# The weights of q and of the output projection: split into high and low halves beside the Fourier transform instead of ahead of it, through DRAM

## Chip, core and metric

One NeuronCore of a Trainium2 chip runs the whole kernel. The metric is the time of one execution on the device, in microseconds (us); lower is better. Engines are named as in the profile: PE is TensorE, DVE is VectorE, ACT is ScalarE, POOL is GpSimd, SP is the engine whose queue issues nearly all DMAs. Every engine works through its own instruction list strictly in order, so an instruction that waits holds up all that stand behind it on the same engine.

## What is computed

One layer of a hybrid block over 2048 latent tokens of width 1024 (a Fourier branch and a retention branch beside each other). Cut to what matters:

```python
h = modulate(rms_norm(x, g_pre), shift, scale)            # shift, scale, gate from silu(c) @ w_ada
f_in, f_gate, q, k, v, r_gate = split(h @ w_in)           # six projections of 512 columns each
q, k = axial_rotary(q) * QK_SCALE, axial_rotary(k)
ret = bidirectional_retention(q, k, v, decay, fwd_state, bwd_state)     # chunks of 128 tokens
mixed = real(fft2(f_in per group of 128 channels)); yf = (mixed @ w_fourier) * silu(f_gate)
yr = group_norm(ret) * gn_gain * silu(r_gate)
out = x + gate * rms_norm(concat(yf, yr) @ w_out, g_post)
```

## The kernel before

The latent tokens are 16 chunks of 128 (c = 0 to 15), two to a tile (t = 0 to 7). Products need more precision than one pass of PE gives, so every operand x is split into hi (x rounded, a copy on ACT) and lo (x - hi, a subtraction on DVE, some on POOL), and a product is three matmuls: hi\*hi, hi\*lo, lo\*hi (`proj_kt`, lines 180 to 182). Splitting a weight costs a load, an ACT copy and a subtraction; a split weight is twice as large as the raw one.

The program runs in stages:

- **Tiles 1 to 7** (about 75 to 320 us): k, v and, for tiles 1 to 3, r_gate of each chunk; k^T, v and the running state go to DRAM (`d_st`). The order within this stage is a scheduler's. Work that is not urgent is put between the chunks by hand: `gate_acc` (the sum over c for the output gate, GG), `decay_tables`, the splits of the Fourier weights (`jobs`: B11, B21, T1, T2, then T3, B22, T4), and `w_ahead`: twelve pieces of the weights of q and of the output projection (`wq`, `wo0`, `wo1`) are loaded, split and stored split in DRAM (`d_w`), two pieces after each of the chunks 2 to 7. So they are done with tile 3.
- **`f_tile` 0 to 7** (320 to 495 us): f_in and f_gate by a Strassen-like scheme of seven products for each pair of chunks. PE's order is written by hand. `h_raw` loads a pair's rows, `h_comb` adds and splits them. In `f_tile(4)` `gate_fin` finishes GG with two matmuls.
- **The transform** (495 to 580 us): order written by hand on all engines. Four classes k of four groups g: `T` (`cls_T`, 12 matmuls into pT) and `Y` (`cls_y`, 6 matmuls, then the gating on POOL). ACT makes Th and DVE makes Tl of each T, which Y reads. Between them PE is filled with `fill`: quarters (6 matmuls) of the r_gate projection of the chunks 15 down to 8, which `rg_rest` generates; their operands (`rgh`) come from DRAM into the four buffers of pool `w4`, so a chunk's load waits until an earlier chunk is done. `pull` issues steps of the next class's operands (`ops_pair`, `ops_even`).
- **q and retention** (from 576 us): q of tile 7 and 6 (`q_steps`), retention of chunk 15, 14, ..., then in `chunk_step` one chunk after the other with the output projection two chunks behind (`out_steps`: o[0], o[1] with `wo0`; o[2], o[3] with `wo1`). `load_sd` fetches k^T, v and states of a chunk, `spill` writes the gated Fourier rows of a group to DRAM. `w_get` loads the split `wq` (before tile 7's q) and `wo0`, `wo1` (between the steps).

Tiles share pools: `units` (20 buffers of 8 KB a partition), `w4` (4 of 4 KB), `w2` (16 of 2 KB, taken by `wk`). A new tile waits until all readers of its buffer's last owner are done, and on SP such a wait holds every DMA behind it.

Of the kernel before, what the change touches and what calls it, by code (L numbers as in the profile page):

```python
# [15 lines left out]
P = 128  # L16
# [15 lines left out]
def hymba_kernel(ctx: ExitStack, tc: tile.TileContext, a: dict, out: bass.AP):  # L32
# [805 lines left out]

    d_w = {n: drm.tile([4, P, 2, 2, 512], F32, name=f"d_{n}") for n in ("wq", "wo0", "wo1")}
    gains = [None] * 4 + [gn_col[:, i:i + 1] for i in range(4)]  # L840

    def w_ahead(n, u):
        src, col = {"wq": (a["w_in"], 1024), "wo0": (a["w_out"], 0), "wo1": (a["w_out"], 512)}[n]
        raw = w4.tile([P, 2, 512], F32, tag="w4", name="wa")
        nc.sync.dma_start(out=raw, in_=src[u * 256:(u + 1) * 256, col:col + 512]
                          .rearrange("(k p) n -> p k n", p=P))
        d = unit([P, 2, 2, 512], F32R, "wahl")
        if n == "wq" or u < 2:
            hl_split(d, raw)
        else:  # L850
            for j in range(2):
                w_split([d], j, raw[:, j, :], gains[2 * u + j])
        nc.sync.dma_start(out=d_w[n][u], in_=d.bitcast(F32))

    def w_get(n, wu, us=range(4)):
        for u in us:
            nc.sync.dma_start(out=wu[u].bitcast(F32), in_=d_w[n][u])

    ahead = [(n, u) for n in ("wq", "wo0", "wo1") for u in range(4)]

    jobs = {(4, 1): [lambda: b_plain("B11", 0, 0)], (5, 1): [lambda: b_plain("B21", 1, 0)],
            (6, 0): [b_T1], (6, 1): [b_T2]}

    for t in range(1, NT - 1):
        hi, lo = hls.pop(t)
        for b in range(2):
# [19 lines left out]
            for n, u in ahead[:2]:  # L886
                w_ahead(n, u)
            ahead = ahead[2:]
# [7 lines left out]
    toks = [slice(b * P, (b + 1) * P) for b in range(2)]  # L896
    b_T3()
# [8 lines left out]
    h_comb(0)  # L906
# [60 lines left out]
    def f_tile(t):  # L967
# [35 lines left out]
        if t == 4:  # L1003
            gate_fin()
# [405 lines left out]
    def rg_load(c):  # L1410
        rgh[c] = [w4.tile([P, KT, P], F32R, tag="w4", name="rgh") for _ in range(2)]
# [36 lines left out]
    with tc.manual_schedule(engines={ENG.PE, ENG.DVE, ENG.Activation, ENG.Pool, ENG.SP}):  # L1448
# [5 lines left out]
        fg_sum(NT - 1, 0, Z, last["u2"])  # L1454
        bg.append(gen1(ops_pair(2)))
        pull(9)
        for g in range(4):
            sg.append(unit([P, SEQ], F32, f"sg{g}"))
            for c in FB[NT - 1]:
                s_ = slice((c - 7) * P, c * P)  # L1460
                nc.sync.dma_start(out=sg[g][:, s_], in_=d_sg[g][:, s_])
        fill(4)
        fg_T(NT - 1, 1)
        fg_T(NT - 1, 0)
        fill(2)
# [3 lines left out]
        bg.append(gen1(ops_pair(1)))  # L1469
# [20 lines left out]
        pull(9)  # L1490
        load_h(7, 0)
        load_h(7, 1)
        load_tab(3)
        load_sd(N1)
        dec.append(wk([P, NH, P], "DT"))
        dec.append(unit([P, 2, NH, P], F32, "dec"))
        nc.sync.dma_start(out=dec[0], in_=d_dec[:, 0])
        nc.sync.dma_start(out=dec[1], in_=d_dec[:, 1:3])
        load_h(6, 0)
        load_h(6, 1)  # L1500
        for g in range(4):
            pend.append((2, g, T(2, g)))
            Y(*pend.pop(0))
            pull(1)
            if g == 0:
                bg.append(gen1(ops_even()))
        for f in q_steps(7):
            if pend:
                Y(*pend.pop(0))
            f()  # L1510
            pull(1)
        pull(9)
# [3 lines left out]
        split_h(6, 1)
        load_sd(N1 - 1)
        wo_u = [w_units(f"wo{j}") for j in range(2)]
        q2 = q_steps(6)
# [200 lines left out]
```

## Time and profile before

| | us |
|---|---|
| median of three runs | 938.44 (937.55 to 939.31) |
| the profiled execution, its own time | 939.14 |
| its span, first to last instruction | 937.3 |
| PE busy | 888.9 (95%) |
| VectorE, ScalarE, GpSimd busy | 583.6, 353.8, 280.4 |

The span and the instruction times are those of one execution under the profiler; its own time is 1.84 us more than its span. PE is busy for 95% of it, so what can be won without changing the arithmetic is PE's idle time and the time in which PE was granted the lower clock.

### The profile page before, as it was taken

The page shows a single profiled execution, that of the slowest core. Times are in us where ns is not written, and L with a number is a line of the kernel's source. Part 1 is how long each engine was busy: PE and PEld are TensorE (multiplying, and loading weights), DVE is VectorE, ACT ScalarE, POOL GpSimd, SP SyncE. Part 2 cuts the span into 40 slices and gives each one's busy share as a digit, 9 for nine tenths or more (in the row PEclk, how much of TensorE's full clock was granted, in tenths as well). Part 3 has the DMA queues.
Part 4 walks back from the last instruction along what each step waited for, and adds up shares of the span by engine and source line. Part 5 has one row for each costly group of instructions (what it writes and reads, how often), then busy time and mean ns, then how long its engine had stood idle before and what let it go on. Part 6 is the DMA issues. An engine that isn't in the chain of part 4 may idle for free.

```text
span 937.3 us, 13777 instructions
## 1 busy us (share of the span) xinstructions
PE 888.9 (95%) x4996; PEld 760.0 (81%) x4996; DVE 583.6 (62%) x1126; ACT 353.8 (38%) x691; POOL 280.4 (30%) x333
## 2 busy tenths in 40 slices
PE   7899999999998799999998899987999999999997
PEld 6678888888787678887886789976898989989885
DVE  3555675585799795476527254773666867677552
ACT  3444754344644553333323233221234233433331
POOL 2106321321456310000001147442343424334342
PEclk8899999999999999999999899999999999999999
DMA  8938987999999732234269589599445464243412
GB/s 303 389 121 328 337 314 299 389 381 391 357 377 371 224 113 68 79 85 118 79 229 355 153 268 413 195 359 381 155 146 180 162 188 170 91 147 113 168 58 90
DMA packets 109939, 214.25 MB, mean 229 GB/s; under 512 B 7728, under 2 KB 58160, under 8 KB 99248
## 3 DMA queue, kind: packets, MB, share of 16 engines
q1 hardware_dynamic: 108000, 207.08, 62.2%
q0 software_dynamic: 576, 4.19, 1.2%
q10 hardware_dynamic: 1296, 2.10, 0.6%
q8 instruction: 39, 0.64, 0.3%
q14 instruction: 28, 0.23, 0.1%
HBM read 141.78 MB, written 71.57 MB: 228 GB/s over the span
## 4 chain that ended last, share of the span: by engine, by line
PE 54%; DMA 7%; DVE 3%; POOL 2%; issue 2%; ACT 0%; SPq 0%; DVEq 0%; POOLq 0%; ACTq 0%
PE pX L926 8%; PE pout L180 6%; PE pout L182 6%; PE pout L181 6%; PE pZ L926 4%; PE pq L1203 3%; PE pq L1204 3%; PE pq L1205 3%; DMA wo<-d_wo 3%; PE pY L926 2%; DMA sd<-d_st 2%; PE psc L1245 2%; PE pr L182 2%; DMA rgh<-d_hl 1%; PE pr L180 1%
## 5 line engine op out<-in xcount | busy, mean ns | idle before, releaser
L180 PE MATMUL pout<-wo,y 128*128 128x512 f32 x256 | 103.0, 402 | 5.7 <-DMA wo<-d_wo 5.7
L182 PE MATMUL pout<-wo,y 128*128 128x512 f32 x256 | 100.4, 392 | 0.0
L181 PE MATMUL pout<-wo,y 128*128 128x512 f32 x256 | 100.2, 391 | 0.0
L1203 PE MATMUL pq<-hq,wq 128*128 128x256 f32 x256 | 74.2, 290 | 0.4 <-DMA hq<-d_hl 0.4
L1204 PE MATMUL pq<-hq,wq 128*128 128x256 f32 x256 | 73.3, 286 | 0.0
L1205 PE MATMUL pq<-hq,wq 128*128 128x256 f32 x256 | 73.2, 286 | 0.0
L926 PE MATMUL pX<-T,S 128*128 128x512 f32 x276 | 67.4, 393 | 1.5 <-DVE fg L58 1.5
L242 POOL TENSOR_TENSOR vd<-v,dk 128x256 f32<-128x256 f32 x64 | 54.0, 872 | 42.6 <-ACT v L634 21.8
L180 PEld LDWEIGHTS pout<-wo,y 128*128 128x128 f32 x256 | 48.3, 189 | 16.8 <-DMA wo<-d_wo 7.8
L206 POOL TENSOR_TENSOR ka<-ka,kb 128x512 f32<-128x512 f32 x16 | 31.4, 1966 | 102.0 <-DVE kb L58 87.5
L926 PEld LDWEIGHTS pX<-T,S 128*128 128x128 f32 x276 | 51.1, 188 | 12.3 <-DVE fg L58 1.9
L182 PEld LDWEIGHTS pout<-wo,y 128*128 128x128 f32 x256 | 48.3, 189 | 10.6
L1335 ACT ACTIVATE t<-pout 128x512 f32<-128x512 f32 x32 | 19.1, 597 | 98.6 <-PE pout L182 71.7
L181 PEld LDWEIGHTS pout<-wo,y 128*128 128x128 f32 x256 | 48.5, 189 | 9.0
L1203 PEld LDWEIGHTS pq<-hq,wq 128*128 128x128 f32 x256 | 50.0, 195 | 0.8 <-issue 0.6
L1204 PEld LDWEIGHTS pq<-hq,wq 128*128 128x128 f32 x256 | 50.0, 195 | 0.2
L1205 PEld LDWEIGHTS pq<-hq,wq 128*128 128x128 f32 x256 | 49.9, 195 | 0.0
L1363 POOL TENSOR_TENSOR xo<-xo,t 128x512 f32<-128x512 f32 x30 | 43.2, 1455 | 21.5 <-DMA xo<-in_x 10.2
L1038 POOL DMA_DIRECT2D tab<-in_tabs x4 | 2.6, 643 | 151.5 <-PE pX L926 151.5
L180 PE MATMUL pv<-wv,hhix 128*128 128x512 f32 x112 | 44.8, 400 | 0.0
L180 PE MATMUL pk<-wk,hhix 128*128 128x512 f32 x112 | 44.1, 393 | 0.0
L182 PE MATMUL pk<-wk,hlox 128*128 128x512 f32 x112 | 43.6, 391 | 0.2 <-DVE hlox L55 0.2
(316 smaller groups left out, 2432.0 us busy)
## 6 DMA issues: line engine op xcount, KB each, us to landing
sd<-d_st SPq DMA_DIRECT2D x16, 1024.0 KB, 6.3
braw<-in_w_in SPq DMA_DIRECT2D x18, 512.0 KB, 8.4
ada<-in_ada_ss SPq DMA_DIRECT2D x8, 1024.0 KB, 12.9
d_wo<-wahl SPq DMA_DIRECT2D x8, 1024.0 KB, 10.3
hr<-d_h SPq DMA_DIRECT2D x32, 256.0 KB, 4.4
rgh<-d_hl SPq DMA_DIRECT2D x16, 512.0 KB, 8.2
wo<-d_wo SPq DMA_DIRECT2D x8, 1024.0 KB, 10.2
out<-xo SPq DMA_DIRECT2D x32, 256.0 KB, 2.1
```

Source lines behind the costliest of these rows:

```text
L180: mm(o, hi[:, kt, tok], whi, start=first, stop=False)
L181: mm(o, hi[:, kt, tok], wlo, start=False, stop=False)
L182: mm(o, lo[:, kt, tok], whi, start=False, stop=last)
L206: nc.gpsimd.tensor_tensor(out=ra, in0=ra, in1=rb.rearrange("p h a f -> p h (a f)"), op=ALU.add)
L242: nc.gpsimd.tensor_tensor(out=t[:, :, i, :], in0=v[:, hs, :], in1=d[:, hs].unsqueeze(2).to_broadcast([P, 2, P]), op=ALU.mult)
L926: mm(o, A[:, x, kt, :], w, start=(first and kt + i == 0), stop=(kt + i == 5), skip_group_check=not first)
L1203: mm(o, whi, h[:, 0, kt % 4], start=(kt == 0), stop=False)
L1204: mm(o, wlo, h[:, 0, kt % 4], start=False, stop=False)
L1205: mm(o, whi, h[:, 1, kt % 4], start=False, stop=(kt == KT - 1))
L1245: mm(psc[:, h * P:(h + 1) * P], sd[:, 0, h, :], qt[h // 2][:, h % 2, tok], start=True, stop=True)
L1335: nc.scalar.activation(ch.t[j], ch.po[j], AF.Square, scale=1.0 / 32.0, accum_out=ch.ss[:, j:j + 1])
L1363: nc.gpsimd.tensor_tensor(out=xo, in0=xo, in1=ch.t[j], op=ALU.add)
```

## The change

- `w_ahead` and `w_get` and the DRAM copy `d_w` go. A generator `w_steps` loads the raw weight in eight pieces of 128x512, two ahead, and splits each into the units that PE reads: ACT the hi part, POOL the lo part of odd pieces without a gain, DVE the others. It is pulled for `wq` in the classes k = 1 to 3 of the transform, for `wo0` behind q of tile 7, for `wo1` in the first `chunk_step`.
- All four classes now stand before q of tile 7 and 6. `fill(1)` and `fill(2)` alternate after each T (before: `fill(3)` in the first two classes, none later), and Y runs one T behind, not two.
- r_gate's loads come in a new order: chunk 13 gets a buffer of its own and is loaded before the gates `sg`, chunk 12 right behind it; 11, 10, 9, 8 when 14, 12, 11, 10 are done.
- In the tiles: `decay_tables` moves from t = 4 to t = 1, `gate_acc` from t = 3, 4 to 2, 3, the Fourier weights' splits one or two chunks earlier; in the last tile the rows of `f_tile(0)` (`h_raw(0)`, `h_comb(0)`) are loaded and combined ahead of the last weights.
- `gate_fin`'s loads and its memset are issued in `f_tile(4)`, its matmuls in `f_tile(5)`.

```diff
+    def gate_prep():
+        gfs.append(wk([P, P], "ones"))
+        nc.vector.memset(gfs[0], 1.0)
...
-    jobs = {(4, 1): [lambda: b_plain("B11", 0, 0)], (5, 1): [lambda: b_plain("B21", 1, 0)],
-            (6, 0): [b_T1], (6, 1): [b_T2]}
+    jobs = {(4, 0): [lambda: b_plain("B11", 0, 0)], (4, 1): [lambda: b_plain("B21", 1, 0)],
+            (5, 1): [b_T1], (6, 1): [b_T2]}
...
-            for n, u in ahead[:2]:
-                w_ahead(n, u)
-            ahead = ahead[2:]
...
+    h_raw(0)
     b_T3()
...
+    h_comb(0)
     b_plain("B22", 1, 1)
-    h_raw(0)
...
+                    for x in {15: (12,), 14: (11,), 12: (10,), 11: (9,), 10: (8,)}.get(c, ()):
+                        rg_load(x)
...
+        rg_load(NCH - 3, True)
         bg.append(gen1(ops_pair(2)))
-        pull(9)
-        for g in range(4):
-            sg.append(unit([P, SEQ], F32, f"sg{g}"))
...
+        pull(2)
         fill(4)
+        fg_tiles()
         fg_T(NT - 1, 1)
         fg_T(NT - 1, 0)
+        pull(9)
...
+        def w_steps(wu, src, col, gs=None, before=2):
+            raws = {}
+            def load(kt):
+                raws[kt] = wk([P, 512], "wraw")
+                nc.sync.dma_start(out=raws[kt], in_=src[kt * P:(kt + 1) * P, col:col + 512])
+            for kt in range(before):
+                load(kt)
+            yield 1
+            for kt in range(KT):
+                if kt + before < KT:
+                    load(kt + before)
+                g = gs[kt] if gs else None
+                w_split(wu, kt, raws.pop(kt), g, gp_ if kt % 2 and g is None else nc.vector)
+                yield 1
...
+        for k in range(4):
+            if k == 0:
+                bg.append(gen1(ops_pair(1)))
+            if k == 1:
+                bg.append(gen1(ops_pair(5)))
+                load_tab(2)
+                bg.append(w_steps(wq_u, a["w_in"], 1024))
...
             for g in range(4):
                 pend.append((k, g, T(k, g)))
-                if len(pend) > 2:
+                fill(1 + g % 2)
+                if len(pend) > 1:
                     Y(*pend.pop(0))
-                fill(3)
                 pull(2)
...
+        bg.append(w_steps(wo_u[0], a["w_out"], 0, gains))
+        q7[0]()
+        Y(*pend.pop(0))
+        pull(1)
+        q7[1]()
...
-            plan = ["P", o[0], "B-", o[1], "A", q[0], q[1], "B", "C", o[2], "B'", o[3]]
+            plan = ["P", o[0], "B-", o[1], "A", "w3", q[0], "w9", q[1], "B", "C", o[2], "B'", o[3]]
```

DVE where tile 7 ends and `f_tile(0)` begins. `ka`, `kb` are the rotary of k of chunk 14 and 15, `T_...` the lo parts of the Fourier weights T2 (2941, 2942) and T3 (2956, 2957) before, T3 (2882) in the change; `A_...`, `S_...` are operands of `f_tile(0)`. Before:

```order
L58 TENSOR_TENSOR ka<-pk,cs 128x512
L58 TENSOR_TENSOR kb<-pk,cs 128x512
L227 SCALAR_TENSOR_TENSOR Sf<-Sf,dk,pkv 128x128 x2
L58 TENSOR_TENSOR braw<-braw,T_2817 128x1024
L227 SCALAR_TENSOR_TENSOR Sf<-Sf,dk,pkv 128x128 x2
L55 TENSOR_TENSOR T_2942<-braw,T_2942 128x1024
L58 TENSOR_TENSOR braw<-braw 128x1024
L55 TENSOR_TENSOR klo<-ka,khi 128x512
L55 TENSOR_TENSOR T_2956<-braw,T_2956 128x1024
L55 TENSOR_TENSOR vlo<-vd,vhi 128x512 x2
L58 TENSOR_TENSOR hs_3127<-hr_3077,hr_3079 128x512
```

and in the change:

```order
L55 TENSOR_TENSOR T_2882<-braw,T_2882 128x1024
L55 TENSOR_TENSOR A_2990<-hr_2868,A_2990 128x512
L58 TENSOR_TENSOR ka<-pk,cs 128x512
L58 TENSOR_TENSOR kb<-pk,cs 128x512
L55 TENSOR_TENSOR A_2991<-hr_2870,A_2991 128x512
L227 SCALAR_TENSOR_TENSOR Sf<-Sf,dk,pkv 128x128 x4
L55 TENSOR_TENSOR S_2993<-hr_2874,S_2993 128x512
L58 TENSOR_TENSOR hs_2988<-hr_2872,hr_2874 128x512
```

The last of T2 and all of T3 have moved ahead of chunk 15's rotary, and the operands of `f_tile(0)` stand directly around it; six instructions of 128x1024 have left the stretch behind `kb`.

SP at the head of the transform. `wr` is r_gate's weight, `d_hl_149` holds the chunks 15 and 14, `d_hl_148` 13 and 12, `d_hl_147` 11 and 10, `d_hl_146` 9 and 8. Before:

```order
L1413 DMA rgh<-d_hl_149 128x8x128
L1078 DMA ccs<-in_ccs 128x256
L1079 DMA wfa<-in_wf 128x512
L1461 DMA sg_4522<-d_sg 128x896 x2
L1461 DMA sg_4525<-d_sg 128x896 x2
L1461 DMA sg_4528<-d_sg 128x896 x2
L1461 DMA sg_4531<-d_sg 128x896 x2
L1413 DMA rgh<-d_hl_148 128x8x128 x4
L1413 DMA rgh<-d_hl_147 128x8x128 x4
L1413 DMA rgh<-d_hl_146 128x8x128 x4
L857 DMA wq_5034<-d_wq 128x2048
```

and in the change:

```order
L1065 DMA wfa<-in_wf 128x512
L1403 DMA rgh<-d_hl_148 128x8x128 x4
L1436 DMA sg_4458<-d_sg 128x896 x2
L1436 DMA sg_4461<-d_sg 128x896 x2
L1436 DMA sg_4464<-d_sg 128x896 x2
L1436 DMA sg_4467<-d_sg 128x896 x2
L1403 DMA rgh<-d_hl_147 128x8x128 x4
L1403 DMA rgh<-d_hl_146 128x8x128 x2
L1478 DMA wraw<-in_w_in 128x512 x5
L1403 DMA rgh<-d_hl_146 128x8x128 x2
L1478 DMA wraw<-in_w_in 128x512 x3
```

The chunks 13 and 12 now stand ahead of the eight loads of `sg`, and the raw pieces of `wq` stand between and behind the last chunks of r_gate, where before the split `wq` stood behind them all.

ACT in the classes k = 1 and 2 of the change. `Th` is the hi part of a T, `p_sb` belongs to a Y, `ope_...` are operands of the last class; before, the rows with `wq_...` were not there and the others stood in the same alternation:

```order
L1109 COPY p_sb<-pp 128x256
L144 CAST wq_4547<-wraw 128x512
L1095 CAST Th<-pT 128x512
L1109 COPY p_sb<-pp 128x256
L1017 CAST ope_4991<-R_3169 128x512 x2
L1017 CAST ope_4996<-R_3169 128x512 x2
L1095 CAST Th<-pT 128x512
L1109 COPY p_sb<-pp 128x256
L144 CAST wq_4547<-wraw 128x512
L144 CAST wq_4548<-wraw 128x512
L1095 CAST Th<-pT 128x512
```

What moved here is the split itself: ACT now waits for a raw piece's load between the Th that PE's next Y needs.

## Rows read from the trace of the kernel before

**Rows 1.** The page: busy time of PE (share of the span, instructions), and the clock that PE was granted in 40 equal slices of the span (tenths of full speed, 9 is 90% or more).

```profile
PE 888.9 (95%) x4996; PEld 760.0 (81%) x4996; DVE 583.6 (62%) x1126; ACT 353.8 (38%) x691; POOL 280.4 (30%) x333
...
PEclk8899999999999999999999899999999999999999
```

**Rows 2.** The list of PE's waits over the whole span, longest first: what waited, for whom, us in total, times, longest.

```profile
PE pout L180 <- DMA wo<-d_wo: 5.7, 5, 3.4
PE pX L926 <- ACT A L541: 4.7, 1, 4.7
PE pr L182 <- DMA rgh<-d_hl: 4.6, 1, 4.6
PE pkT L508 <- POOL ka L206: 4.3, 2, 2.6
PE psc L1245 <- DMA sd<-d_st: 3.5, 1, 3.5
...
PE pr L180 <- DMA rgh<-d_hl: 2.3, 1, 2.3
PE pX L926 <- DVE fg L58: 1.5, 1, 1.5
...
PE pg L819 <- DVE ones L812: 1.0, 1, 1.0
PE psc L1245 <- POOL qt L1222: 0.9, 2, 0.5
```

**Rows 3.** Stretches of the span: bounds and length in us, then busy us and instructions of PE, PEld, DVE, ACT, POOL, the mean granted clock, the mean busy share of the 16 DMA engines, GB/s. The second lies within the first: from the rotary of chunk 15 to the first sum of `f_tile(0)`.

```profile
300.00:349.00 49.00, 42.34 (x192) 34.03 (x190) 42.53 (x59) 24.80 (x42) 12.78 (x11) 0.93 0.61 194
...
307.28:344.02 36.74, 31.54 (x142) 25.36 (x141) 33.32 (x46) 21.55 (x37) 10.63 (x9) 0.91 0.56 176
...
525.00:570.00 45.00, 45.00 (x265) 39.93 (x264) 21.29 (x35) 16.01 (x31) 18.30 (x18) 1.00 0.77 257
...
610.00:655.00 45.00, 35.83 (x226) 31.41 (x225) 23.40 (x65) 9.54 (x22) 15.22 (x23) 0.93 1.01 373
```

**Rows 4.** The same view for the four stretches in the middle of the span in which the granted clock was half.

```profile
324.00:330.80 6.80, 5.74 (x13) 3.95 (x14) 6.40 (x6) 5.38 (x9) 4.50 (x4) 0.50 0.59 177
515.00:522.00 7.00, 3.45 (x8) 2.77 (x9) 0.00 (x0) 0.00 (x0) 0.00 (x0) 0.51 0.78 231
627.80:631.20 3.40, 3.40 (x10) 2.85 (x11) 0.00 (x0) 0.58 (x2) 0.62 (x1) 0.50 1.15 348
651.70:658.50 6.80, 5.99 (x28) 6.03 (x29) 4.55 (x9) 1.24 (x2) 0.88 (x1) 0.50 0.71 275
```

**Rows 5.** Instructions in order of time (start, us, engine, line, what it does; in brackets its engine's idle time before it and what ended that), and one line of POOL's waits in 300 to 349 us (us in total, times, longest).

```profile
244.36 0.66 PE L508 MATMUL pkT<-ident,ka 128*128 128x128 f32 x4 [1.61 <-POOL ka L206]
...
294.91 0.66 PE L508 MATMUL pkT<-ident,ka 128*128 128x128 f32 x4 [2.64 <-POOL ka L206]
...
323.32 1.04 ACT L541 CAST T<-braw 128x1024 fp32r<-128x1024 f32 x1 [0.76 <-DMA hr<-d_h]
...
POOL vd L242 <- DMA d_st<-kT: 8.4, 1, 8.4
```

**Rows 6.** The chain of work that ended last, three of its pieces: start, us, what; a DMA runs from its issue to its landing.

```profile
504.48 14.03 DMA rgh<-d_hl
...
613.62 14.04 DMA wo<-d_wo
...
635.79 16.58 DMA sd<-d_st
```

**Rows 7.** The transform. Four matmuls of T: the first two stand at the same place of two neighbouring steps with `fill(3)`, the last two at the same place of two steps without a fill. Then two groups of instructions in 500 to 575 us: line, engine, operation, count, busy us, mean ns of one, idle before and its releaser.

```profile
536.53 0.28 PE L1100 MATMUL pT<-tab,op 128*128 128x256 f32 x1
542.79 0.28 PE L1100 MATMUL pT<-tab,op 128*128 128x256 f32 x1
...
569.15 0.28 PE L1099 MATMUL pT<-tab,op 128*128 128x256 f32 x1
...
571.31 0.28 PE L1099 MATMUL pT<-tab,op 128*128 128x256 f32 x1
...
L55 DVE TENSOR_TENSOR Tl<-pT,Th 128x512 fp32r<-128x512 f32 x11 | 7.6, 690 | 29.7 <-ACT Th L1109 29.7
...
L1109 ACT CAST Th<-pT 128x512 fp32r<-128x512 f32 x11 | 6.4, 586 | 20.5 <-PE pT L1101 20.1 <-ACT rg L640 0.4
```

**Rows 8.** Duration of one instruction in ns, min/median/max, first and last start in us, shapes: the split of r_gate's weight in eight pieces of 128x512 (ACT hi, DVE lo, POOL lo), and the rotary's sum on POOL.

```profile
L144 ACT CAST wr<-wrr x8: 604/634/645, 69.6 to 77.4; 128x512 fp32r<-128x512 f32 x8
L150 DVE TENSOR_TENSOR wr<-wrr,wr x6: 678/1102/1524, 72.3 to 79.8; 128x512 fp32r<-128x512 f32 x6
L150 POOL TENSOR_TENSOR wr<-wrr,wr x2: 1294/1294/1295, 70.8 to 75.1; 128x512 fp32r<-128x512 f32 x2
...
L206 POOL TENSOR_TENSOR ka<-ka,kb x16: 1263/1296/7783, 83.3 to 307.4; 128x512 f32<-128x512 f32 x16
```

**Rows 9.** DMA issues: what, queue, count, KB each, median us from issue to landing.

```profile
wrr<-in_w_in SPq DMA_DIRECT2D x8, 256.0 KB, 7.2
...
xo<-in_x SPq DMA_DIRECT2D x30, 256.0 KB, 4.2
...
hx<-d_h SPq DMA_DIRECT2D x14, 512.0 KB, 8.3
```

More of the change, by code (lines that the diff above doesn't have):

```diff
@@ L877, in hymba_kernel @@
                 x_prep(t + 1)
-            if t == 4 and b == 0:
+            if t == 1 and b == 0:
                 decay_tables()
-            if t in (3, 4):
-                gate_acc(4 * (t - 3) + 2 * b)
-                gate_acc(4 * (t - 3) + 2 * b + 1)
+            if t in (2, 3):
+                gate_acc(4 * (t - 2) + 2 * b)
+                gate_acc(4 * (t - 2) + 2 * b + 1)
             if t == 1 and b == 1:
@@ L1003, in f_tile @@
         if t == 4:
+            gate_prep()
+        if t == 5:
             gate_fin()
@@ L1408, in hymba_kernel, with rg_load @@
     wfs, last, rgh, sg = [], {}, {}, []
-    def rg_load(c):
-        rgh[c] = [w4.tile([P, KT, P], F32R, tag="w4", name="rgh") for _ in range(2)]
+    def rg_load(c, own=False):
+        if own:
+            u = unit([P, 2, KT, P], F32R, "rgh")
+            rgh[c] = [u[:, 0], u[:, 1]]
+        else:
+            rgh[c] = [w4.tile([P, KT, P], F32R, tag="w4", name="rgh") for _ in range(2)]
         for i in range(2):
@@ L1438, in hymba_kernel, with fg_tiles @@
     rg_gen = rg_rest()
+    def fg_tiles():
+        for g in range(4):
+            sg.append(unit([P, SEQ], F32, f"sg{g}"))
+            for c in FB[NT - 1]:
+                s_ = slice((c - 7) * P, c * P)
+                nc.sync.dma_start(out=sg[g][:, s_], in_=d_sg[g][:, s_])
     def fill(n):
@@ L1468, in hymba_kernel @@
         load_tab(1)
-        bg.append(gen1(ops_pair(1)))
         def T(k, g):
@@ L1490, in hymba_kernel @@
[L1490 to L1498, printed above, removed]
+            if k == 1:
+                assert len(ops[5]) == 2
+        q7, q2 = q_steps(7), q_steps(6)
         load_h(6, 0)
         load_h(6, 1)
[L1501 to L1512, printed above, removed]
+        bg.append(w_steps(wo_u[0], a["w_out"], 0, gains))
[3 more added lines that the diff above has]
+        q7[1]()
+        split_h(6, 0)
+        split_h(6, 1)
+        q7[2]()
+        pull(2)
+        q7[3]()
+        spill(0)
+        spill(1)
+        load_sd(N1 - 1)
         rets[N1] = retention(N1)
         next(rets[N1])
-        split_h(6, 0)
@@ L1516, in hymba_kernel @@
[L1516 to L1519, printed above, removed]
+        q2[0]()
+        next(rets[N1])
+        pull(2)
+        q2[1]()
+        next(rets[N1])
         def y15_split(g):
@@ L1561, in hymba_kernel @@
         next(rets[N1 - 1])
-        spill(2)
-        spill(3)
-        w_get("wo1", wo_u[1])
+        wo1 = w_steps(wo_u[1], a["w_out"], 512, gains)
+        next(wo1)
     qn = {}
@@ L1596, in chunk_step @@
                 split_yf(co)
+            elif f[0] == "w":
+                for _ in range(int(f[1])):
+                    next(wo1, 0)
             elif f[0] == "F":
```

101 lines of the change are left out of this document (35 added, 66 removed).

## The prediction

> **What bounds the kernel now.** I read the page first. PE is busy for 888.9 of 937.3 us [rows 1], and the change issues the same matmuls as before, so only PE's 48.4 us of idle time and the stretches at half clock can move. The slices of granted clock [rows 1] are full nearly everywhere. Four short stretches in the middle stand at 0.50 or 0.51, which is the lower of the two levels (1.2 GHz), and each lies inside or right behind a wait of PE [rows 4]. Work at half the clock takes twice the time, so half of PE's busy time there is lost: 5.74/2 = 2.9, 3.45/2 = 1.7, 3.40/2 = 1.7 and 5.99/2 = 3.0 us, together 9.3.
>
> The list of PE's waits says for whom it waits in the parts that the change touches [rows 2]: 5.7 us for the split `wo`, 4.7 and 1.5 for operands of `f_tile(0)`, 4.6 and 2.3 for an `rgh` chunk, 4.3 for `ka` ahead of two transposes of k, 3.5 for `sd`, 1.0 for the memset of `ones`. The rest of the 48.4 us is mostly the start and the end, which the change leaves alone.
>
> The stretches tell what lies behind two of these. From 307.28 to 344.02 VectorE is busy for 33.32 of 36.74 us [rows 3]: the wait for `f_tile(0)` is VectorE's. From 610 to 655 the DMA engines are full (1.01, 373 GB/s) while PE works for 35.83 of 45 us [rows 3]: the waits for `wo` and `sd` are the DMA's. The chain shows the same transfers landing 14.03 (`rgh`), 14.04 (`wo`) and 16.58 us (`sd`) after issue [rows 6].
>
> **The change, part by part.** The sum is made against the profiled execution, 939.1 us, which is 0.7 above the median of 938.4.
>
> *GG and the Fourier weights earlier.* The first wait for `ka` is 1.61 us at 244.36 [rows 5], in tile 5, where `gate_acc` fills VectorE ahead of `ka`'s products; it moves to tiles 2 and 3, whose VectorE loses the twelve split pieces. I take all of it as gone: **1.6** (bounds 0 and 1.6). The second, 2.64 at 294.91 [rows 5], goes with the one rotary sum that took 7783 ns on GpSimd, where the median is 1296 [rows 8]; VectorE runs wide subtractions of the Fourier weights at that time, and does so after the change too. It stays. `decay_tables` moves to t = 1 at nothing: ScalarE is busy for 38% of the span [rows 1]; uncovered it would cost no more than the 1.6 of this item.
>
> *Start of `f_tile(0)`.* It costs 4.7 + 1.5 idle and 2.9 of clock, 9.1. Six VectorE operations of 128x1024 leave the stretch; 128x512 takes 0.68 to 1.5 us with its median at 1.10 [rows 8], so twice the size is 1.2 to 2.2, say 1.4: 8.2 us of 33.3. That leaves 25 of some 30 us, so the operands should be ready. What is late next: GpSimd waits 8.4 us for a `w2` buffer for v of chunk 15, freed by the store of k^T [rows 5]. That store doesn't come earlier by as much as PE does, so part of the wait reaches PE's product of k and v. I leave 4 of 9.1: **5.1** (bounds 2 and 9.1).
>
> *Gate.* The memset now stands a tile ahead of its matmuls: **1.0** (bounds 0 and 1.0).
>
> *`rgh` in a new order.* Before, chunk 13 waits for a buffer and lands behind eight `sg` loads of 0.46 MB: 4.6 + 2.3 idle and 1.7 of clock, 8.6. Now 13 (own buffer) and 12 stand ahead of `sg`; `sg` is read by the last tile's gating, off PE's path. I leave 0.5: **8.1** (bounds 3 and 8.6). Later chunks have a lead. A bare step takes 571.31 - 569.15 = 2.16 us, one with three quarters 542.79 - 536.53 = 6.26 [rows 7], so a quarter is 4.10/3 = 1.37. The transform becomes 16 x 2.16 + 24 x 1.37 = 67 us, 4.2 a step with 1.5 quarters. Chunk 10 is issued when 12 is done, and only chunk 11 (four quarters, 11.2 us) lies between, against 8.3 us for a DMA of this kind [rows 9] and 14.03 at worst [rows 6]. On SP the loads behind such a wait are held too: the last pieces of `wq` and then `h`, `sd`, `hx`.
>
> *The splits.* From tiles 2 to 7 go twelve loads of 0.5 MB and twelve stores of 1 MB; PE did not wait for them there, so that alone gives nothing. Late, 12 MB of split loads become 6 MB of raw pieces: 6.3e6 B / 373 GB/s = 16.9 us of DMA time, more than the 5.7 + 3.5 idle and 1.7 + 3.0 clock (13.9) that the full queues cost now. I leave 2.5, since `hx` and `sd` still crowd 590 to 640: **11.4** (bounds 5 and 13.9).
>
> The work of a split now stands beside the transform: 24 pieces of one ScalarE copy (0.634 us) and one subtraction, 0.68 to 1.5 on VectorE, 1.29 on GpSimd [rows 8]. Before, in 525 to 570, VectorE was busy for 21.29, ScalarE for 16.01, GpSimd for 18.30 of 45 us at full PE [rows 3], for seven steps: 3.0, 2.3 and 2.6 a step. With a piece a step it is at most 4.1, 2.9 and 3.9 of 4.2 us: they fit, barely. But ScalarE and VectorE work in order, and behind a piece that has not landed stand the `Th` (586 ns) and `Tl` (690 ns) [rows 7] that Y needs. Y begins 2.16 + 1.5 x 1.37 = 4.2 us after its T on average, so about 2.9 us of delay are free. A raw piece of 256 KB lands in 7.2 us at the start and 4.2 in the tiles [rows 9]; it is issued two pieces ahead, which is one to two steps, 4.2 to 8.4 us. Only the first pieces, held on SP behind chunk 9, should show: I take **-1.5** (bounds 0 and -10).
>
> Sum: 1.6 + 5.1 + 1.0 + 8.1 + 11.4 - 1.5 = 25.7, and 939.1 - 25.7 = **913** us.
>
> **Rivals.**
>
> *All hidden.* No wait is left in these places: 1.6 + 9.1 + 1.0 + 8.6 + 13.9 = 34.2, so 905. For it: 67 us for 16 steps leave every engine some room. Against: PE 8 us early meets transfers that haven't moved.
>
> *Waits move on.* The product for chunk 15 waits the full 8.4 us (4 more than forecast), and chunk 10 of r_gate lands 14.0 us after issue against its lead of 11.2 (2.8, and 1.7 of clock): 913 + 8.5, about 921. For it: both latencies are in the rows. Against: 14.03 was measured behind 3.7 MB of `sg`, which now lie elsewhere.
>
> *GpSimd blocked.* One rotary sum took 7783 ns where 1296 is the median, and VectorE's split ranged from 678 to 1524 [rows 8]. If each of `wq`'s four GpSimd pieces were stretched that way (6.5 us each, 26 in all), GpSimd, which has 1.6 us a step to spare, would make up some 8 of it over the five steps in which these pieces lie, and 18 would reach Y's gating and PE: 913 + 18 = 931. Against: GpSimd's two pieces of `wr` took 1294 and 1295 ns beside VectorE's six, and of sixteen sums the median is 1296.
>
> The Trainium skill ("SBUF — State Buffer", section "Who interferes with whom") says that a VectorE instruction with two SBUF inputs and a GpSimd instruction that reads SBUF contend for a shared port pair, which the one holds for a whole instruction while the other blocks. By that rule a split on both engines at once, which is what this change adds, gains nothing from the second. The trace agrees as far as the one sum of 7783 ns goes, and not where GpSimd's two pieces of `wr` stood beside VectorE's.
>
> *Slower: ScalarE held by raw pieces.* Each of the 24 copies stands in order ahead of a Th, a p_sb or a rotary's input. If a piece lands 7.2 us after an issue only one step (4.2) ahead, it holds ScalarE for 3.0, at worst 24 x 3.0 = 72 us on PE: 939.1 - 27.2 + 72 = 984. It decides from 27.2/24 = 1.1 us a piece: above that the change is slower. For it: SP's queue holds the pieces behind waits for `w4` buffers, and no row shows a raw load in this stretch, where the DMA engines are already 0.77 busy [rows 3]. Against: 2.9 us of each delay are free, a held piece leaves the next one already landed, and the split loads of `wq` no longer share the queues.
>
> *Nothing.* The DMA engines stay the bound from 610 to 655 and the wait at `f_tile(0)` is taken up by v of chunk 15: 8.1 + 1.0 + 1.6 gained and as much lost to held pieces, 938.
>
> **How the numbers follow.** Forecast (907 to 918) 0.52; all hidden 0.13; waits move on 0.22; GpSimd blocked 0.05; slower 0.05; nothing 0.03. The likeliest is 913. From 901 (all hidden, and 4 us more than its sum) to 926 (waits moved on, with 5 us more of held pieces) lies all but GpSimd blocked, slower and nothing, 0.13, and some 0.05 of the tails. A measurement of this kernel tells about 0.2%, 1.9 us, from no change. Faster by more than that: 0.92; within: 0.03; slower: 0.05.
>
> **What would show it.** In the changed profile PE's list has no wait for `wo`, none for `ones`, one instead of two for `ka`; the operands of `f_tile(0)` cost under 4 us, any rest stands at a product with v of chunk 15; no wait for `rgh` at chunk 13 and, if waits move on, one at chunk 10. The granted clock stays full from 500 to 640, and the DMA's share in the stretch of the first output projections falls below 1. Y's matmuls wait for Th, Tl less than 2 us in all; many waits there that follow a copy of `wq` on ScalarE would make the forecast wrong on the slow side, and so would subtractions of `wq` on GpSimd far above 1.3 us. PE busy should fall by the clock's share, some 5 to 8 us.

## The result, and the profile after

The changed kernel takes **924.13 us** (median of four runs, 922.18 to 925.53) against 938.0 before: ratio 0.9851, 95% interval 0.9828 to 0.9874. It is 13.9 us faster; the forecast was 25 faster. The time lies inside the range (901 to 926), 11 us above the likeliest value. The profiled execution took 924.31 us, with a span of 922.5 (before: 937.3).

The page after, PE's busy time and the granted clock in 40 slices, for [rows 1]:

```profile
PE 887.0 (96%) x4996; PEld 760.0 (82%) x4996; DVE 587.9 (64%) x1126; ACT 354.7 (38%) x699; POOL 290.4 (31%) x341
...
PEclk7899999999999999999999999999999999999999
```

PE's idle time fell from 48.4 to 922.5 - 887.0 = 35.5 us, by 12.9, and its busy time, with the same matmuls, by 1.9. So nearly all of the gain is idle time, and the clock gave back much less than the 5 to 8 us that were forecast.

The list of PE's waits after, whole span (waited for, us in total, times, longest), for [rows 2]:

```profile
...
PE pkv L256 <- DVE vlo L55: 4.2, 3, 3.2
...
PE pkT L508 <- POOL ka L206: 2.6, 1, 2.6
PE po L1263 <- DVE qfT L58: 2.4, 2, 2.1
PE pT L1087 <- POOL op L1019: 2.0, 3, 0.9
PE pT L1085 <- ACT op L1017: 1.7, 2, 0.9
...
PE pyT L1296 <- POOL on L1290: 1.0, 1, 1.0
PE psc L1231 <- DVE qt L1208: 0.9, 2, 0.5
```

No line is left for `wo`, `sd`, `rgh`, `ones` or an operand of `f_tile(0)`. In their place stand `vlo` (v of chunk 15, just ahead of `f_tile(0)`'s second product), `op` (the operands of the transform's next class) and `qfT` (the decayed q of chunk 14). Neither of the last two was in the forecast.

The stretches of before and the four half-clock stretches, after (bounds, length, busy us of PE, PEld, VectorE, ScalarE, GpSimd, clock, DMA share, GB/s), for [rows 3, 4]:

```profile
525.00:570.00 45.00, 43.17 (x260) 38.71 (x261) 26.89 (x44) 21.10 (x42) 31.40 (x31) 0.96 0.72 241
...
610.00:655.00 45.00, 41.76 (x263) 37.23 (x264) 32.62 (x84) 13.25 (x26) 17.60 (x19) 0.96 0.74 258
```

```profile
267.40:270.82 3.42, 3.40 (x11) 2.82 (x12) 3.42 (x5) 1.20 (x3) 3.42 (x3) 0.57 1.07 413
332.10:335.52 3.42, 3.42 (x12) 2.83 (x13) 3.42 (x5) 1.43 (x2) 0.00 (x0) 0.59 0.05 15
544.20:547.62 3.42, 3.40 (x10) 2.82 (x11) 0.82 (x3) 1.04 (x3) 2.21 (x3) 0.52 1.09 355
612.10:615.52 3.42, 3.36 (x17) 3.36 (x18) 3.34 (x8) 1.04 (x1) 1.70 (x2) 0.57 1.15 347
```

The DMA engines are no longer full from 610 to 655 (0.74 where it was 1.01). Half clock still follows four waits: for `ka`, `vlo`, `op` and `qfT`. Each such stretch costs about half of its 3.4 us, 1.7, or 6.8 in all, against 9.3 before.

By place, in the profiled executions (idle time of PE from the lists, plus half of the busy time at half clock):

| place | before | after | gained | forecast |
|---|---|---|---|---|
| tiles and start of `f_tile(0)`, 240 to 350 us | 11.3 + 2.9 | 6.9 + 3.4 | 3.9 | 6.7 |
| gate | 1.0 | 0 | 1.0 | 1.0 |
| r_gate and transform | 6.9 + 1.7 | 3.9 + 1.7 | 3.0 | 6.6 |
| first output projections | 9.2 + 4.7 | 4.5 + 1.7 | 7.7 | 11.4 |
| q of tile 7 and 6 | 2.1 | 0.9 | 1.2 | 0 |
| first 75 us | | 0.8 idle and about 1 of clock more | -1.8 | 0 |

The sum is 15.0, of a difference of the spans of 14.8.

### The profile page after: what moved, and what is told of

Its sections match the earlier page's. It is cut to its first block, busy times and chain, and to the rows that moved or that the text cites. A ratio compares the mean times of both kernels' runs of the same rounds, so it can differ in the third digit from the quotient of the medians.

```text
span 922.5 us, 13765 instructions
## 1 busy us (share of the span) xinstructions
PE 887.0 (96%) x4996; PEld 760.0 (82%) x4996; DVE 587.9 (64%) x1126; ACT 354.7 (38%) x699; POOL 290.4 (31%) x341
## 4 chain that ended last, share of the span: by engine, by line
PE 79%; DVE 8%; DMA 4%; issue 3%; ACT 3%; POOL 2%; SPq 0%; DVEq 0%; ACTq 0%; POOLq 0%
PE pX L910 9%; PE pout L180 6%; PE pout L182 6%; PE pout L181 6%; PE pZ L910 5%; PE pr L180 3%; PE pr L181 3%; PE pr L182 3%; PE pq L1191 2%; PE pq L1190 2%; PE pq L1189 2%; PE pY L910 2%; PE pk L182 2%; PE pv L180 2%; PE pk L180 2%
## 5 line engine op out<-in xcount | busy, mean ns | idle before, releaser
L1189 PE MATMUL pq<-hq,wq 128*128 128x256 f32 x256 | 73.2, 286 | 0.0
L1190 PE MATMUL pq<-hq,wq 128*128 128x256 f32 x256 | 72.4, 283 | 0.0
L1191 PE MATMUL pq<-hq,wq 128*128 128x256 f32 x256 | 72.4, 283 | 0.0
L242 POOL TENSOR_TENSOR vd<-v,dk 128x256 f32<-128x256 f32 x64 | 51.6, 835 | 44.2 <-ACT v L634 25.4
L910 PEld LDWEIGHTS pX<-T,S 128*128 128x128 f32 x276 | 52.4, 192 | 10.9
L182 PEld LDWEIGHTS pout<-wo,y 128*128 128x128 f32 x256 | 48.0, 188 | 10.3
L1190 PEld LDWEIGHTS pq<-hq,wq 128*128 128x128 f32 x256 | 49.1, 192 | 0.2
L1189 PEld LDWEIGHTS pq<-hq,wq 128*128 128x128 f32 x256 | 49.1, 192 | 0.2
L1191 PEld LDWEIGHTS pq<-hq,wq 128*128 128x128 f32 x256 | 49.1, 192 | 0.0
```

What stands on the lines that cost most here:

```text
L182: mm(o, lo[:, kt, tok], whi, start=False, stop=last)
L242: nc.gpsimd.tensor_tensor(out=t[:, :, i, :], in0=v[:, hs, :], in1=d[:, hs].unsqueeze(2).to_broadcast([P, 2, P]), op=ALU.mult)
L910: mm(o, A[:, x, kt, :], w, start=(first and kt + i == 0), stop=(kt + i == 5), skip_group_check=not first)
L1189: mm(o, whi, h[:, 0, kt % 4], start=(kt == 0), stop=False)
L1190: mm(o, wlo, h[:, 0, kt % 4], start=False, stop=False)
L1191: mm(o, whi, h[:, 1, kt % 4], start=False, stop=(kt == KT - 1))
```

## The experiments

Each ratio is to the kernel before on the same chip; its 95% interval is about 0.002 (1.8 us) to either side, and that of a difference of two ratios about 0.003 (2.8 us). "Over the changed kernel" is the difference of the ratios to 0.9851, times 938.

**One part undone at a time.** First r_gate's order:

```diff
-                    for x in {15: (12,), 14: (11,), 12: (10,), 11: (9,), 10: (8,)}.get(c, ()):
-                        rg_load(x)
+                    if c - 2 >= 2 * RG:
+                        rg_load(c - 2)
...
-        rg_load(NCH - 3, True)
...
+        fg_tiles()
         fill(4)
-        fg_tiles()
```

> The changed kernel with r_gate's loads in the old order: sg's eight loads first, chunk c-2 loaded when chunk c is done, no buffer of its own for chunk 13. Theory (the parts of the change gain separately, this one what the trace shows as gone: 2.3 + 4.6 us of idle PE and 1.7 of clock): 8.6 us slower than the changed kernel, about 932.7, and PE waits about 7 us for rgh at chunk 13. Rival (the order gains only together with the rest, the wait moves on to another transfer): less than 3 us slower, and the list of waits shows no rgh or another wait gone in exchange.

Measured: 930.4 us, 0.9922 [0.9903, 0.9941], 6.7 over the changed kernel. The size is near the theory's, the waits are not. PE's list of this kernel:

```profile
PE pT L1087 <- POOL op L1019: 2.6, 3, 0.9
PE pT L1085 <- ACT op L1017: 2.6, 3, 0.9
...
PE pr L182 <- DMA rgh<-d_hl: 1.0, 1, 1.0
```

Only 1.2 us of wait for `rgh` came back, not 7; a likely reason, not tested, is that the transform's new order of `fill` gives chunk 13 more time. The waits for `op` grew by 1.5. Half clock now held through most of 507 to 515 (0.57, some 3 us lost), where the changed kernel has none, but the changed kernel's own stretch at 544 is gone. From 490 to 580 us this run loses 2.7 us more of idle time and about 1.5 more of clock, and 1.5 more of idle time at the output projections.

The same order alone, put into the kernel before:

> The kernel before with nothing but the new order of r_gate's loads: chunk 13 in a buffer of its own ahead of sg, 12 behind 15, 11 behind 14, 10, 9, 8 behind 12, 11, 10. Theory (the wait for rgh is a cost of its own): 2.3 + 4.6 us of idle and 1.7 of clock go, 8.6 us faster than before, 929.5. Rival (PE then meets wo and sd earlier, whose loads fill the DMA engines, and waits there for what it gained): less than 4 us faster, with longer waits for wo, sd or hq.

Measured: 931.7 us, 0.9924 [0.9903, 0.9945], 7.1 faster than before. Its list of PE's waits:

```profile
PE pout L180 <- DMA wo<-d_wo: 5.9, 4, 3.8
...
PE psc L1245 <- DMA sd<-d_st: 3.5, 1, 3.5
```

No wait for `rgh` is left, and those for `wo` and `sd` are 5.9 and 3.5 where they were 5.7 and 3.5 [rows 2]: PE comes earlier and so do the loads, so nothing was eaten. The rival falls.

The splits, put back behind the chunks 2 to 7 and through DRAM (`w_ahead` and `d_w` as before, the split halves loaded where the raw pieces stood):

```diff
+            for n, u in ahead[:2]:
+                w_ahead(n, u)
+            ahead = ahead[2:]
...
-        def w_steps(wu, src, col, gs=None, before=2):
+        def w_steps(wu, n):
+            for u in range(4):
+                w_get(n, wu, (u,))
+                yield 1
+                yield 1
```

> The changed kernel with the weights of q and of the output projection split ahead again in tiles 2 to 7 and stored in DRAM; in the places where the pieces stood the split halves are loaded. Theory (late DMA volume): the waits for wo and sd are back, about 9 us, the DMA engines are full in the stretch of the first output projections, the wait for qfT (2.1) and its clock loss are gone: 7.7 us slower than the changed kernel, about 932. Rival (the full DMA of before came from what else stood there, the late spills and h loads, which the new order spreads): less than 3 us slower.

Measured: 934.6 us, 0.9954 [0.9934, 0.9973], 9.7 over the changed kernel. Its list of PE's waits:

```profile
PE pk L180 <- ACT hhix L132: 6.0, 2, 4.0
PE pout L180 <- DMA wo<-d_wo: 5.2, 3, 2.6
PE pkv L255 <- ACT vhi L245: 4.3, 2, 2.8
```

The wait for `wo` is back and that for `qfT` gone, as expected; `sd` is not back. But the larger part stands in the tiles, where the forecast had priced the splits at nothing: 10.3 us for `hhix` and `vhi`, which the changed kernel has not, against 6.8 there for `vlo` and `ka`. The last split piece is done at 236 us, ahead of these waits, so it is not the work of the splits itself that holds PE there. The profiled execution (931.55 us) is one of the faster of ten, 930.97 to 937.13.

This run also tells what the smaller volume is worth at the output projections. The stretch of [rows 3] in it:

```profile
610.00:655.00 45.00, 39.76 (x259) 35.25 (x258) 23.95 (x64) 10.97 (x26) 14.65 (x16) 0.89 0.90 335
```

The DMA engines are fuller again (0.90 where the changed kernel has 0.74), and yet PE doesn't wait for `sd`. From 580 to 720 us PE is idle for 10.9 us in the kernel before, 5.6 in the changed one and 5.2 here, and the clock takes 4.7, 1.7 and about 4 more: 15.6, 7.3 and 9. So in these executions only some 2 of the 8 us need the smaller volume; the rest, the wait for `sd` included, came with the other parts of the change, the new places of the loads among them. Which of them did it wasn't tested.

The tile stage, put back into its old order:

```diff
-    jobs = {(4, 0): [lambda: b_plain("B11", 0, 0)], (4, 1): [lambda: b_plain("B21", 1, 0)],
-            (5, 1): [b_T1], (6, 1): [b_T2]}
+    jobs = {(4, 1): [lambda: b_plain("B11", 0, 0)], (5, 1): [lambda: b_plain("B21", 1, 0)],
+            (6, 0): [b_T1], (6, 1): [b_T2]}
...
-    h_raw(0)
     b_T3()
...
-    h_comb(0)
     b_plain("B22", 1, 1)
+    h_raw(0)
...
+    h_comb(0)
```

> The changed kernel with the tile stage in its old order: decay_tables at t = 4, gate_acc at t = 3 and 4, the Fourier weights' splits and the rows of f_tile(0) where they stood before. The splits of q's and the output's weights stay out of it. Theory (VectorE's order at 244 us and at f_tile(0) made the waits): 1.6 for ka, and 4.7 + 1.5 at f_tile(0) with its half clock against what is left there now (3.2 + 0.8 + 1.7): about 4 us slower than the changed kernel, 928. Rival (VectorE was late there only because it also split the twelve pieces of q and the output): no change within 1 us, PE's list without a wait for A at f_tile(0).

Measured: 934.1 us, 0.9959 [0.9944, 0.9974], 10.1 over the changed kernel, more than either expected. The wait for `A` did not come back; PE waits for the operands of v instead:

```profile
PE pkv L256 <- DVE vlo L55: 6.7, 3, 2.6
PE pkv L255 <- ACT vhi L245: 2.8, 2, 1.6
```

In the tiles the forecast had 6.7 us for the two parts together; undone alone, each costs more than that in all. Hence both at once:

> The changed kernel with both undone: the split of q's and the output's weights ahead in tiles 2 to 7 (as e2_split_ahead) and the old order of the tile stage (as e3_old_tiles). Alone they cost 10.5 and 9.9 us over the changed kernel. Theory (the two are coupled: the new order of the tile stage fills the time that the splits had, and the old order leaves chunk 14 and 15 short whatever was split before): well under the sum of 20.4, about 10 to 13 us over the changed kernel, 934 to 937. Rival (independent parts): 20 us over it, 944.

Measured: 929.5 us, 0.9897 [0.9874, 0.9921], only 4.3 over the changed kernel, less than either one alone, and less than the theory had. So 9.7 of the 13.9 us that the whole change won are there with both parts undone: they come of the others, r_gate's order, the transform's and the gate's, and of the new places of the split loads. From 580 to 720 us this run loses about 9 us, as the one with the splits alone put back. One stretch, 240 to 350 us, of five kernels shows it. The kernel before, the changed one, splits put back, old order put back, both (columns as above):

```profile
240.00:350.00 110.00, 98.73 (x470) 80.52 (x469) 95.69 (x134) 59.65 (x105) 48.07 (x38) 0.97 0.82 288
```

```profile
240.00:350.00 110.00, 103.12 (x489) 85.80 (x488) 95.91 (x138) 50.81 (x84) 40.98 (x35) 0.97 0.73 254
```

```profile
240.00:350.00 110.00, 98.98 (x452) 81.96 (x451) 87.33 (x124) 49.67 (x84) 37.20 (x36) 0.92 0.84 298
```

```profile
240.00:350.00 110.00, 98.94 (x462) 82.13 (x461) 93.88 (x131) 53.87 (x90) 39.86 (x35) 0.94 0.72 252
```

```profile
240.00:350.00 110.00, 98.35 (x469) 80.33 (x468) 95.47 (x133) 59.61 (x106) 48.08 (x38) 0.97 0.83 291
```

PE is idle for 11.3, 6.9, 11.0, 11.1 and 11.7 us, and at a mean clock of 0.97, 0.97, 0.92, 0.94 and 0.97 its busy time loses 3.0, 3.1, 7.9, 5.9 and 3.0 more: 14.2, 10.0, 18.9, 17.0 and 14.6. Over the changed kernel that is 4.3 for before, 9.0, 7.0 and 4.6, which accounts for most of what the three mixtures cost, and for less than a third of the 13.9 us between the kernel before and the changed one. VectorE is not busier in the two slow mixtures (87.33 and 93.88) than in the changed kernel (95.91), so their waits are of order, not of load. Which choice of the scheduler makes them wasn't followed further and stays open.

**The wait for `op`.** In the changed kernel, on ScalarE, the copies of the next class's operands (L1017) stand two behind each Y:

```profile
518.65 0.37 ACT L1109 COPY p_sb<-pp 128x256 f32<-128x256 f32 x1 [0.40 <-ACT rg L640]
521.07 0.62 ACT L1017 CAST op<-bt 128x512 fp32r<-128x512 f32 x1 [2.05 <-DVE bt L58]
523.05 0.62 ACT L1017 CAST op<-bt 128x512 fp32r<-128x512 f32 x1 [1.36 <-DVE bt L58]
523.58 0.58 ACT L1095 CAST Th<-pT 128x512 fp32r<-128x512 f32 x1
```

Each step is a chain over VectorE, ScalarE and back, 2.0 us long, and the last pair starts behind the third step's `p_sb`. With steps of 6.3 us that was early enough; with 4.2 it is not.

```diff
-                pull(2)
+                pull(2 if k > 1 else 3 if g < 2 else 1)
```

> The changed kernel with the operands of the next class made one step earlier: three steps are pulled behind each of the first two T of the classes k = 0 and 1 and one behind the others, instead of two behind each. Theory (PE's new waits at 522 to 525 and 542 to 545 come from operands whose copies and subtractions start behind the gating of the third step): these waits, 3.9 us, and 1.7 of clock behind them go: 5.6 us faster than the changed kernel, about 918.5. Rival (VectorE, ScalarE and GpSimd are full beside the shorter steps, so what is pulled earlier makes Th, Tl or Y late instead): within 1.5 us of the changed kernel, with new waits of PE for Th or Tl.

Measured: 918.9 us, 0.9800 [0.9782, 0.9818], 4.8 below the changed kernel. Waits for `op` are 0.3 us, and Th and Tl together cost 0.9:

```profile
PE pp L1105 <- ACT Th L1095: 0.6, 1, 0.6
...
PE pp L1106 <- DVE Tl L55: 0.3, 1, 0.3
...
PE pT L1087 <- POOL op L1019: 0.3, 1, 0.3
```

The engines had room; only the start was late. The theory holds.

**The wait for `qfT`.** VectorE of the changed kernel ahead of it:

```profile
604.49 0.16 DVE L1285 SCALAR_TENSOR_TENSOR gnb<-mv,grs 128x4 f32<-128x4 f32 x1 [0.68 <-POOL grs L79]
606.89 3.27 DVE L152 SCALAR_TENSOR_TENSOR wo<-wraw,vec,wo 128x512 fp32r<-128x512 f32 x4 [2.24 <-ACT wo L146]
610.09 0.75 DVE L58 TENSOR_TENSOR qfT<-qt,dec 128x256 f32<-128x256 f32 x2
```

The raw pieces had landed; the four subtractions wait for ScalarE's copies, which stand behind chunk 15's normalization, and take 2.2 + 3.3 us ahead of `qfT`.

```diff
-        pull(9)
         rets[N1 - 1] = retention(N1 - 1)
...
             y15_split(g)
+        pull(9)
```

> e4_ops_ahead, and the last four pieces of wo0 (kt 4 to 7) split behind chunk 15's y instead of between the scores of chunk 14 and its decayed q. Theory (PE's wait for qfT, 2.14 us at 604, and the half clock behind it come from four subtractions on VectorE, 3.3 us, that stand ahead of qfT and wait for ScalarE's copies behind chunk 15's normalization): these 2.1 and 1.7 go, nothing new for wo: 3.8 us below e4_ops_ahead, about 915. Rival (the pieces are needed by the output projection right behind, so the wait moves to pout): within 1 us of e4_ops_ahead, with a wait of PE for wo of 2 us or more.

Measured: 916.5 us, 0.9756 [0.9731, 0.9782], 4.1 below the run before it by the ratios (2.4 by the medians). The wait for `qfT` fell from 2.1 to 0.3, but a new one came, for `wo1`:

```profile
PE pout L180 <- ACT wo L144: 2.7, 1, 2.7
```

```profile
615.31 1.15 ACT L144 CAST wo<-wraw 128x512 fp32r<-128x512 f32 x2
623.43 1.24 ACT L144 CAST wo<-wraw 128x512 fp32r<-128x512 f32 x2 [6.96 <-DMA wraw<-in_w_out]
```

Here ScalarE is held for 6.96 us by a raw piece that hasn't landed, and PE sees it: the mechanism of the forecast's slower rival, once in 24 pieces. Both theories have a part: the wait for `qfT` went as the first says, and one moved to `pout` as the second says, for another weight than it named. How much of the 4.1 us is this edit's isn't shown: in the profiled executions PE's idle time from 580 to 720 us fell only from 5.6 to 5.0, with one stretch of half clock in each, and some 2 us less were lost in the first 75 us, which the edit leaves alone.

**The wait for `ka`.** GpSimd's sum in the changed kernel, and VectorE beside it:

```profile
261.91 5.46 POOL L206 TENSOR_TENSOR ka<-ka,kb 128x512 f32<-128x512 f32 x1 [5.44 <-issue]
```

```profile
261.70 1.21 DVE L58 TENSOR_TENSOR braw<-braw 128x1024 f32<-128x1024 f32 x1
262.83 2.28 DVE L55 TENSOR_TENSOR hlox<-xtx,hhix 128x2048 fp32r<-128x2048 f32 x1
265.03 1.21 DVE L55 TENSOR_TENSOR T<-braw,T 128x1024 fp32r<-128x1024 f32 x1
```

```diff
...
-        return rotary(p1, cs_load(c))
+        return rotary(p1, cs_load(c), nc.vector if c in (10, 11, 12, 13) else None)
```

> e5_ops_wo0, and the rotary's sum of k for the chunks 10 to 13 on VectorE instead of GpSimd. Theory (the sum that takes 5.5 us instead of 1.3 on GpSimd is blocked by VectorE's subtractions with two operands in SBUF, and PE's wait for ka, 2.1 to 2.6, is its price, with 1.7 of half clock behind it): wait and clock go, about 3.9 us below e5_ops_wo0, about 911. Rival (GpSimd's record is rough and PE waits because VectorE itself is late with ka's products): the wait for ka stays above 1.5 us, same time within 1 us.

Measured: 916.7 us, 0.9755 [0.9729, 0.9781]: no change. The sum takes 0.67 to 1.10 us on VectorE and the wait for `ka` is gone, so the slow sum was its cause; but the time isn't gained. VectorE is now late for the next products, and PE's list from 230 to 350 us has:

```profile
PE pkv L256 <- DVE vlo L55: 4.7, 2, 2.5
PE pk L182 <- DVE hlox L55: 1.2, 2, 0.8
```

**`vlo` of chunk 15.** It is `vd` less `vhi`. In the changed kernel ScalarE is done with `vhi` at 328.42; VectorE, whose order has a subtraction for T4 ahead of `vlo`, waits 1.59 us for that weight and starts `vlo` 2.9 us later:

```profile
327.81 0.61 ACT L245 CAST vhi<-vd 128x512 fp32r<-128x512 f32 x1
```

```profile
329.08 1.23 DVE L58 TENSOR_TENSOR braw<-braw,T 128x1024 f32<-128x1024 f32 x1 [1.59 <-DMA braw<-in_w_in]
...
331.34 0.68 DVE L55 TENSOR_TENSOR vlo<-vd,vhi 128x512 fp32r<-128x512 f32 x1
```

Its second half goes to GpSimd:

```diff
...
+            if last and j:
+                nc.gpsimd.tensor_tensor(out=lo, in0=t, in1=hi.bitcast(F32), op=ALU.subtract)
...
```

> e6_ka_dve, and the last subtraction of v of chunk 15 (vlo, second half) on GpSimd instead of VectorE. Theory (the wait of 3.2 us at 331 is VectorE's order: vlo stands behind a sum for T4 whose weight had not landed): the wait falls to about 1 us or less and its half clock goes: 2 to 4 us below e6_ka_dve, about 908. Rival (v of chunk 15 itself is late, through GpSimd's buffer of 3.2 us): the wait stays above 2 us.

Measured: 914.9 us, 0.9736 [0.9710, 0.9761]; 1.8 below the run before it, within the intervals. The wait fell from 2.5 to 1.1, and 1.5 us for `fg`, known from [rows 2], came back behind it, so that PE's idle time from 240 to 350 us did not fall (6.4 before the edit, 6.8 with it). The order was the wait's cause; a gain from mending it isn't shown. This is the fastest version that was run: 2.6% below the kernel before and 1.2% below the changed one.

**Raw pieces, further ahead and less far ahead.**

```diff
-        wo1 = w_steps(wo_u[1], a["w_out"], 512, gains)
+        wo1 = w_steps(wo_u[1], a["w_out"], 512, gains, 5)
```

> e7_vlo_pool, and the raw pieces of wo1 loaded five ahead instead of two. Theory (PE's wait of 1.6 us for wo at 623, 2.7 in the two runs before, is ScalarE held for 5.8 us by a raw piece that was issued only one piece earlier behind full queues): ScalarE's wait for the piece goes, PE's wait for wo with it: 1.6 us, and where the clock fell behind it 1.5 more, below e7_vlo_pool, 912 to 913.5. Rival (the DMA engines are the bound there, an earlier issue only delays sd and yf): same time within 1 us and a wait of PE for sd or y instead.

Measured: 916.2 us, 0.9766 [0.9744, 0.9788]: no gain. ScalarE's wait for `wo1` didn't go, it moved to a later piece (7.1 us), PE's wait for `wo` fell to 0.8, and 1.5 us for `mk` came in exchange. The rival's time is right within the intervals; the wait that it named, for `sd` or `y`, is not there.

```diff
-        def w_steps(wu, src, col, gs=None, before=2):
+        def w_steps(wu, src, col, gs=None, before=1):
```

> The changed kernel with the raw pieces loaded one ahead instead of two, in all three places. Theory (a held copy on ScalarE is covered by some 2.9 us per step, and pieces pulled two in a step hide behind each other): ScalarE waits longer for raw pieces than in the changed kernel (11.5 us in all there), PE hardly: 0 to 4 us slower than the changed kernel. Rival (each held piece reaches PE through Th, p_sb or a rotary): a landing of 5.7 us behind a piece pulled in the same step costs up to 3 us a piece, 24 pieces: 20 us slower or more.

Measured: 927.6 us, 0.9885 [0.9864, 0.9905], 3.2 over the changed kernel. ScalarE's waits for raw pieces from 495 to 660 us, changed kernel, then this one:

```profile
ACT wo L144 <- DMA wraw<-in_w_out: 7.6, 3, 6.9
ACT wq L144 <- DMA wraw<-in_w_in: 3.9, 2, 2.4
```

```profile
ACT wo L144 <- DMA wraw<-in_w_out: 20.0, 3, 11.1
ACT wq L144 <- DMA wraw<-in_w_in: 7.7, 2, 5.4
```

ScalarE is held for 16.2 us more, and 3 of them reach the end. The rival's 20 us fall: ScalarE does stand behind its pieces, but the work it feeds has slack.

## Why the prediction came out as it did

*The places were right, one cause was not.* The waits for `rgh`, `wo`, `sd`, `ones` and the first `ka` went; the second `ka` stayed, at 2.6 us; the rest at `f_tile(0)` stands at v of chunk 14 and 15, nearly as named. "I leave 4 of 9.1" measured 0.8 + 3.2 + 0.2 and 1.7 of clock, 5.9. But the cause that the forecast gave for it, GpSimd's wait for a buffer that the store of k^T frees (8.4 us before), is not there: GpSimd waits 3.3 and 3.2 us for PE, none for the store, and 2.9 of the 3.2 us at chunk 15 are VectorE's order, in which `vlo` stands behind a weight that lands late. Naming that place was in part luck. Two slips in the working change nothing: six times 1.4 us is 8.4 and not 8.2, and twice 0.68 to 1.5 is more than "1.2 to 2.2", while one subtraction of 128x1024 takes 1.2 us in the lines above; and the splits of before stand behind the chunks 2 to 7, which are the tiles 1 to 3, not "tiles 2 to 7".

*First failed step: -1.5 for the transform.* The sum asked whether each engine's busy time fits into a step of 4.2 us and found that it does. It did not follow the chain that a shorter step makes late: the operands of the next class. It measured 3.9 of idle time and 1.7 of clock, and the run with the operands a step earlier gave 4.8 us back. The step's own worry, raw pieces of `wq`, cost PE nothing: ScalarE waited 3.9 us for them and no Th was late.

*Second failed step: 11.4 for the splits' late volume.* The sum put all 13.9 us of waits and clock at the output projections down to the volume of the split loads and left 2.5. What is left measured 4.5 + 1.7: the pieces that moved to this place also stand in VectorE's order, which the sum left out, and the wait for `qfT` fell from 2.1 to 0.3 when `wo0`'s last pieces went behind it. The DMA's share did fall (0.74 instead of 1.01), and the waits for `wo` and `sd` went. But the runs with the splits through DRAM again have no wait for `sd` either and lose about 9 us from 580 to 720, where it was 15.6 before and 7.3 in the changed kernel. So most of the 7.7 us gained here is not shown to be the volume's, and that the sum came as near as it did was in part luck.

*Third: the price of nothing for the splits in the tiles.* The sum, 6.7 for the tile stage against 3.9 to 4.3 measured, missed by some 2.5. Worse was the split into parts: the forecast priced the move of the Fourier weights by itself and the splits' going at nothing. The runs show that either one undone alone leaves the stage 7.0 and 9.0 us above the changed kernel, and both undone only 4.6: the one gains only with the other.

*The clock.* The forecast gave back half clock wherever it removed a wait, and its sign, full clock from 500 to 640, failed at 544 and 612. New waits of 0.9 to 3.2 us brought half clock of their own, one of them (for `ka`) where the same wait before had none. In the first 75 us, which the change leaves alone, half clock was longer in this profile (0.53 over 8 to 19 us, 0.69 before), and PE waited 0.8 us more. The run with only r_gate's order on the kernel before has that longer stretch too, and the one with r_gate's old order in the changed kernel has not, so these 1.8 us belong to no part of the change.

*The rivals.* "All hidden" and "nothing" are out. "Waits move on" named 921, near the result, but of its 8.4 us at v of chunk 15 only 3.2 came, and by another cause, and chunk 10 of r_gate never waited: that its number is near is luck. "GpSimd blocked" was wrong for `wq`: its four pieces on GpSimd took 1277 to 1319 ns (of `wo`'s four, one took 2157). "ScalarE held" happens and costs little.

*The rule and the trace.* What that rival feared for `wq` happened elsewhere: the 5.46 us of `ka` above. The Trainium skill ("SBUF — State Buffer", section "Who interferes with whom") says that of a VectorE instruction with two SBUF inputs and a GpSimd instruction that reads SBUF one blocks until the other is done. The trace agrees as far as the sum is stretched while such subtractions run, and shows more: it lasted through three wide ones and into what followed, not through one instruction. Moving it to VectorE removed the wait and not the time.

## What to carry to other kernels

When steps get shorter because filler work is spread, check the chain that prepares the next stage against the new step length, not only the engines' busy time per step. A piece of work that is moved next to another stage is paid for in every in-order queue it stands in: ask what stands right behind it on each engine, not only whether its data has landed. Parts of a change that a scheduler orders together are not priced one by one: undo them alone and together before giving a gain to either.

## What the runs showed of the hardware

A GpSimd sum of 1.3 us lasted 5.5 to 7.8 us beside a run of wide VectorE subtractions, in the kernel before [rows 8], in the changed one and in the one with both parts undone. Whether PE's clock falls behind a wait of 2 to 3 us was not the same each time: behind 2.6 us for `ka` it fell in the changed kernel (0.57 over 3.4 us) and did not in the kernel before [rows 4, 5]. The run with r_gate's order alone, whose tiles are those of the kernel before, has the same wait of 2.64 us in the same place, and there the clock fell (0.57 from 294 to 302 us, where the kernel before has 1.00). That makes a wait of this size worth its length alone or up to some 3 us more, which is as large as the differences that a single edit here was meant to make.
